# A gated convolution block on one core: y_b's normalization moved behind y_a's last evacuation, and q's lo parts made by ScalarE and an accumulating DMA

## The chip, the cores and the metric

The kernel runs on one core of one Trainium2 chip. The engines named here are TensorE (PE in the profile, its weight loads PEld), VectorE (DVE), ScalarE (ACT), GpSimd (POOL) and SyncE (SP, which only issues DMAs). The metric is the device time of one execution in microseconds; less is better.

## The reference

One layer of a streaming encoder on `x` of 1024 positions by 1024 channels, all in fp32:

- `h` is an RMS norm of `x`, scaled and shifted by a modulation of `c`. One projection of `h` with 7 x 1024 columns gives `b_s, c_s, v_s, v_c, gl_c` and two gates.
- `y_a = (b_s * conv3(c_s * v_s)) @ w_short_out`, with a causal convolution of width 3.
- `u = conv31(v_c * sigmoid(gl_c)) + bias`, then a layer norm over the channels, then `silu`; `y_b = u @ w_conf_out`.
- `x = x + g1 * ((g_a * y_a + g_b * y_b) @ w_o)`, with `g_a`, `g_b` the sigmoids of the gates.
- A second norm and modulation, a SwiGLU feed-forward with 2816 hidden channels, a second residual sum and a last RMS norm.

In the kernel's names `q` is `b_s * conv3(c_s * v_s)`, the operand of y_a, and `zs` is the normalized `silu` that is the operand of y_b.

## The kernel before

Channels lie on the 128 partitions (eight blocks of 128), positions along the free dimension in two halves of 512. The products keep fp32 accuracy by a split: a number is a hi part (rounded to `float32r`) plus a lo part (what the rounding left), and `mm3` issues three matmuls, hi x hi, hi x lo and lo x hi (lines 277, 278 and 280). So every operand is made in two steps: a cast to hi on ScalarE and a subtraction for lo. For weights this is `split_w`: the cast L203, and the lo part L204 on VectorE or, for the window projections and `w_short`, on GpSimd. For activations it is `split` (cast L308, subtraction L309 on VectorE).

The stages, in the order of the program:

1. Norm of `x`, modulation, and a first part of the projection ("lead"), up to about 130 us.
2. The window projections: twelve duals, each two pairs of column blocks for both halves, by seven products (`PRODUCTS`) in place of eight. `win_evac` takes each product out of PSUM. The kinds of a pair are `u` (the GLU), `p` (`c_s * v_s`, then `short_conv`), `q` (b_s times the short convolution) and `g` (gates). VectorE runs the 31-tap convolution (L608) between the evacuations; GpSimd makes the weights' sums (L226 to L230) and lo parts. At the end of each `q` pair, `q_store` runs for two blocks and two halves: ScalarE casts half of `sc[j]` into the first half of a tile `qs` (L491), GpSimd subtracts it to make the lo part in the second half (L492), and SyncE stores `qs` to DRAM (L494). There are four such groups, at about 229 to 248, 331 to 366, 450 to 488 and 547 to 565 us of the span, sixteen stores in all.
3. y_a: for each of eight output blocks `j`, 48 matmuls for both halves; VectorE multiplies each half with its gate into `ma` (L702). Beside it run the layer norm's mean and variance, and `act_b`, which prepares y_b's operand: multiplication with the reciprocal deviation (VectorE, L681), `silu` (ScalarE, L682), and the split (L308, L309).
4. y_b, half by half: `row_blocks` runs over the eight input blocks `k` and keeps eight output blocks open in PSUM, six of the pool `ps`, which y_a uses too, and two of `ps2`. `next_b(k, h)` calls `act_b` one step ahead, and a piece of modulation (L262), whose operand is a DMA of SyncE (`raw<-in_ada`).
5. The output projection "mix", the feed-forward, the last norm.

The order on each engine is fixed when the program is built. The framework's planner goes through the program with estimated times, gives each engine the instruction that is ready and stands earliest in the program, and gives out the slots of the tile pools as they come free. `tc.issue_after(ins)` adds one constraint: what the block issues on the engine of `ins` comes behind `ins` in that engine's order. At run time each engine follows its order and waits where something isn't ready. SyncE's DMAs and GpSimd's DMAs go out in the order of those engines.

`sc`, `qs`, `p`, `u` and the gates' `sig` tiles share the pool `uc`, which has eight slots; a slot is free for the next tile when the last reader of the old one is done.

Of the kernel before, what the change touches and what calls it, by code (L numbers as in the profile page):

```python
# [36 lines left out]
AF = mybir.ActivationFunctionType  # L37
ALU = mybir.AluOpType
# [4 lines left out]
H = 512  # L43
KC = D // P
# [61 lines left out]
def block_kernel(ctx: ExitStack, tc: tile.TileContext, xT, c, vecs, ada, w_first, w_plain, w_duals,  # L106
                 w_short, w_conf, w_o, w_fi, w_fo, w_last, outT):
    nc = tc.nc
# [36 lines left out]
    def s_tile(name, dt=F32):  # L145
        return hl_tile(name, dt)

    def g_tile(name):
        return gsp.tile([P, H], F32, tag="gs", name=name)

    def f32(t):
        return t.bitcast(F32)

    halves = (slice(0, H), slice(H, T))
# [18 lines left out]
    def col(base, k):  # L173
        return vec[:, base + k : base + k + 1]
# [70 lines left out]
    def next_w(ahead=AHEAD):  # L245

        fetch(ahead + 1)
        return ready.pop(0)
# [6 lines left out]
    def modulation(i, raw=None):  # L255

        b = ADA_ORDER[i]
        if raw is None:
            raw = load(ada[i])
        else:  # L260
            nc.sync.dma_start(raw, ada[i])
        nc.vector.tensor_tensor_reduce(  # L262
            out=raw, in0=raw, in1=cs, scale=1.0, scalar=col(V_ADA, b),
            op0=ALU.mult, op1=ALU.add, accum_out=modc(b),
        )
# [16 lines left out]
    def col_block(w, act, hs, name):  # L282

        outs = [ps_tile(f"{name}{h}") for h in hs]
        for k in range(KC):
            mm3(outs, slice(k * P, k * P + P), w, [act[k][h] for h in hs], k == 0, k == KC - 1)
        return outs
# [18 lines left out]
    def split(src, tile_of, name):  # L306
        hi, lo = tile_of(name + "h", dt=F32R), tile_of(name + "l", dt=F32R)
        nc.scalar.copy(hi, src)  # L308
        split.ins = nc.vector.tensor_tensor(lo, src, f32(hi), ALU.subtract).ins  # L309
        return hi, lo  # L310
# [93 lines left out]
    def uc_tile(name, n=T + CK - 1, dt=F32):  # L404
        return ucp.tile([P, T + CK - 1], dt, tag="uc", name=name)[:, :n]
# [78 lines left out]
    sc = [None] * KC  # L484
    q_dram = {}

    def q_store(j):

        for h in range(2):
            s = uc_tile("qs", T, F32R)  # L490
            nc.scalar.copy(s[:, :H], sc[j][:, halves[h]])  # L491
            nc.gpsimd.tensor_tensor(s[:, H:], sc[j][:, halves[h]], f32(s[:, :H]), ALU.subtract)  # L492
            q_dram[j, h] = dram.tile([P, T], F32, name=f"q{j}{h}")
            nc.sync.dma_start(q_dram[j, h], f32(s))  # L494

# [17 lines left out]
    def win_evac(pairs):  # L513
# [15 lines left out]
        def evac(i, m, ps):  # L529
# [22 lines left out]
            elif m == "5":  # L552
                e["z"] = e["c"][1] if kind == "g" else g_tile("z")
                nc.scalar.copy(e["z"], ps)
            elif m == "7":
                plus(e["z"], ps, e["z"])
                if kind in "ug":
                    nc.scalar.activation(e["z"], e["z"], AF.Sigmoid, scale=-1.0)
                elif kind == "q":
                    minus_times(sc[j + 1][:, halves[1]], e["z"], sc[j + 1][:, halves[1]])  # L560
            else:
                if kind in "ug":
                    sig = e["c"][0] if kind == "g" else g_tile("sig")
                    nc.scalar.activation(sig, ps, AF.Sigmoid, scale=-1.0)
                if kind == "u":
                    nc.vector.tensor_tensor(e["b"][0], e["b"][0], sig, ALU.mult)
                elif kind == "p":
                    minus_times(e["b"][0], ps, e["b"][0])
                    short_conv(j, e["p"])
                elif kind == "q":  # L570
                    minus_times(sc[j + 1][:, halves[0]], ps, sc[j + 1][:, halves[0]])
                    for i in range(2):
                        q_store(j + i)
                else:
                    for g, t in zip((j, *rest), e["t"]):
                        nc.scalar.dma_start(gate_dram[g], t)
# [58 lines left out]
    def ln_mean():  # L635
        mu = []
        for h in range(2):
            mps = ps_tile("mu")
            nc.tensor.matmul(mps, ones, tot[h], start=True, stop=True)
            nc.scalar.activation(tot[h], mps, AF.Copy, scale=1.0 / D)  # L640
            mu.append(tot[h])
        return mu
# [3 lines left out]
    def ln_square(j):  # L646
        cv.append(uc_tile(f"cv{j}", T))
        nc.sync.dma_start(cv[j], cv_dram[j])
        for h in range(2):
            nc.vector.tensor_tensor(cv[j][:, halves[h]], cv[j][:, halves[h]], mu[h], ALU.subtract)  # L650
            sq = g_tile("sq")
            nc.scalar.activation(sq, cv[j][:, halves[h]], AF.Square, scale=1.0 / 32.0)
            if j == 0:
                sqs[h] = sq
            else:
                nc.vector.tensor_tensor(sqs[h], sqs[h], sq, ALU.add)

    def ln_rstd(sqs):
        vs, ts = [], []
        for h in range(2):  # L660
            vs.append(ps_tile("var"))
            nc.tensor.matmul(vs[h], ones, sqs[h], start=True, stop=True)
        for h in range(2):
            ts.append(g_tile(f"rl{h}t"))
            nc.scalar.activation(ts[h], vs[h], AF.Ln, bias=eps2)
        return [rstd_end(vs[h], eps2, *exp_half(ts[h], f"rl{h}")) for h in range(2)]
# [11 lines left out]

    def act_b(k, h):
        z = cv[k][:, halves[h]]  # L680
        nc.vector.tensor_tensor(z, z, rl[h], ALU.mult)  # L681
        nc.scalar.activation(z, z, AF.Silu, bias=col(V_LNB, k), scale=col(V_LNG, k))  # L682
        zs[k, h] = split(z, s_tile, "zs")

    def next_b(k, h):

        if (k, h) < (KC - 1, 1):
            act_b(*((k + 1, h) if k < KC - 1 else (0, 1)))
        modulation(24 + KC * h + k)
        return zs[k, h]  # L690
# [5 lines left out]
    ma = {}  # L696
    for j in range(KC):
        for h, ps in enumerate(col_block(next_w(), qT, (0, 1), "ya")):
            ga = g_tile("ga")
            nc.gpsimd.dma_start(ga, gate_dram["a", j][:, halves[h]])  # L700
            ma[j, h] = s_tile(f"ma{j}{h}")
            nc.vector.tensor_tensor(ma[j, h], ps, ga, ALU.mult)  # L702
        if j == 0:
            mu = ln_mean()
        if j < 5:
            for i in range((0, 1, 3, 5, 7)[j], (1, 3, 5, 7, 8)[j]):
                ln_square(i)
        if j == 5:
            rl = ln_rstd(sqs)
        if j == KC - 2:  # L710
            act_b(0, 0)
        if j < KC - 2:
            modulation(16 + j)
# [403 lines left out]
```

## Time and profile before

| | |
|---|---|
| median of 3 runs | 1540.28 us (1537.14 to 1541.44) |
| the profiled execution | 1538.34 us, its span 1536.6 us |
| mean granted TensorE clock | 0.988 |
| TensorE busy | 1470.5 us, 96% of the span |
| VectorE, ScalarE, GpSimd busy | 1182.1, 636.5 and 597.1 us |

A row of the time line gives the start from the beginning of the span, the duration, the engine, the line of the kernel, the operation, the tile written and the tiles read, and the number of instructions merged; in brackets stands the idle time of the engine before it and what ended it. A row of the waits reads: who waited, on whom, microseconds in total, how many times, the longest. A row of the windows gives the stretch, its length, TensorE's busy time and instructions, the granted clock, the share of the DMA engines that was busy, and GB/s. A row by line or tile gives the shortest, median and longest duration in ns, and the first and last start.

### The profile page before, as it was taken

The page shows a single profiled execution, that of the slowest core. Times are in us where ns is not written, and L with a number is a line of the kernel's source. Part 1 is how long each engine was busy: PE and PEld are TensorE (multiplying, and loading weights), DVE is VectorE, ACT ScalarE, POOL GpSimd, SP SyncE. Part 2 cuts the span into 40 slices and gives each one's busy share as a digit, 9 for nine tenths or more (in the row PEclk, how much of TensorE's full clock was granted, in tenths as well). Part 3 has the DMA queues.
Part 4 walks back from the last instruction along what each step waited for, and adds up shares of the span by engine and source line. Part 5 has one row for each costly group of instructions (what it writes and reads, how often), then busy time and mean ns, then how long its engine had stood idle before and what let it go on. Part 6 is the DMA issues. An engine that isn't in the chain of part 4 may idle for free.

```text
span 1536.6 us, 17882 instructions
## 1 busy us (share of the span) xinstructions
PE 1470.5 (96%) x6466; PEld 1206.8 (79%) x6466; DVE 1182.1 (77%) x1559; ACT 636.5 (41%) x894; POOL 597.1 (39%) x493
## 2 busy tenths in 40 slices
PE   4799999999998999999999989999999999999996
PEld 3588887877886888877788868788888888888885
DVE  7987898989998882875975798777767765676756
ACT  6563334333333343244334564444444443212235
POOL 1316788788768884310111101101000016535005
PEclk9999999999999999999999999999999999999998
DMA  9432214223222249754764527544444449999403
GB/s 365 149 103 72 96 56 151 69 97 110 96 69 96 70 175 394 252 185 158 238 208 158 168 80 259 192 151 151 151 152 154 155 151 368 349 297 272 129 14 110
DMA packets 88024, 256.16 MB, mean 167 GB/s; under 512 B 10112, under 2 KB 12288, under 8 KB 87936
## 3 DMA queue, kind: packets, MB, share of 16 engines
q1 hardware_dynamic: 47248, 147.01, 28.4%
q0 software_dynamic: 36944, 95.44, 19.1%
q10 hardware_dynamic: 3744, 12.58, 2.0%
q8 instruction: 50, 0.82, 0.2%
q14 instruction: 38, 0.31, 0.1%
HBM read 188.41 MB, written 66.58 MB: 166 GB/s over the span
## 4 chain that ended last, share of the span: by engine, by line
PE 41%; issue 7%; DVE 2%; DMA 1%; POOL 0%; ACT 0%; DVEq 0%; ACTq 0%; POOLq 0%
PE x L277 6%; PE x L280 6%; PE x L278 6%; PE z L280 3%; PE z L277 3%; PE z L278 3%; PE y L280 2%; PE y L278 2%; PE y L277 2%; PE mix L280 1%; PE mix L278 1%; PE mix L277 1%; PE yb L277 1%; DMA hid<-stage 1%; PE yb L278 1%
## 5 line engine op out<-in xcount | busy, mean ns | idle before, releaser
L203 ACT CAST wh<-raw 128x1024 fp32r<-128x1024 f32 (+2 forms) x260 | 262.0, 1009 | 408.5 <-PE z L278 99.8
L204 POOL TENSOR_TENSOR wl<-raw,wh 128x1024 fp32r<-128x1024 f32 (+1 forms) x95 | 242.7, 2562 | 101.0 <-ACT wh L203 93.2
L204 DVE TENSOR_TENSOR wl<-raw,wh 128x1024 fp32r<-128x1024 f32 (+2 forms) x165 | 189.3, 1148 | 56.0 <-ACT wh L203 53.6
L608 DVE SCALAR_TENSOR_TENSOR c<-diff,vec,c 128x512 f32<-128x512 f32 x248 | 182.3, 750 | 6.4 <-DMA q<-qs 2.6
L868 POOL DMA_DIRECT2D hid<-stage x71 | 37.9, 534 | 352.4 <-DVE stage L317 350.2
L277 PE MATMUL x<-th,wh 128*128 128x512 f32 x336 | 130.7, 389 | 0.0
L278 PE MATMUL x<-tl,wh 128*128 128x512 f32 x336 | 130.7, 389 | 0.0
L280 PE MATMUL x<-th,wl 128*128 128x512 f32 x336 | 130.7, 389 | 0.0
L608 DVE SCALAR_TENSOR_TENSOR c<-u,wsum,c 128x512 f32<-128x512 f32 x112 | 84.0, 750 | 7.1 <-issue 5.1
L277 PE MATMUL x<-t2h,wh 128*128 128x512 f32 x184 | 73.4, 400 | 6.3 <-ACT wh L203 4.5
L280 PE MATMUL x<-t2h,wl 128*128 128x512 f32 x184 | 72.9, 397 | 4.6 <-POOL wl L204 4.1
L262 DVE CUSTOM_DVE_ANT_0 raw<-raw,cs,vec 128x1024 f32<-128x1024 f32 x24 | 34.6, 1444 | 51.2 <-DMA raw<-in_ada 47.0
L277 PEld LDWEIGHTS x<-th,wh 128*128 128x128 f32 x336 | 63.1, 188 | 13.2
L278 PEld LDWEIGHTS x<-tl,wh 128*128 128x128 f32 x336 | 63.1, 188 | 13.1
L280 PEld LDWEIGHTS x<-th,wl 128*128 128x128 f32 x336 | 63.1, 188 | 13.0
L278 PE MATMUL x<-t2l,wh 128*128 128x512 f32 x184 | 72.9, 396 | 0.2
L280 PE MATMUL z<-th,wl 128*128 128x512 f32 x168 | 65.5, 390 | 0.0
L277 PE MATMUL z<-th,wh 128*128 128x512 f32 x168 | 65.4, 389 | 0.0
L278 PE MATMUL z<-tl,wh 128*128 128x512 f32 x168 | 65.4, 389 | 0.0
L316 ACT CAST stage<-g 128x512 fp32r<-128x512 f32 x62 | 38.3, 620 | 60.9 <-DVE g L857 30.4
L894 POOL DMA_DIRECT2D th<-hid x71 | 38.1, 536 | 53.9 <-PE x L280 29.4
L277 PE MATMUL yb<-zsh,wh 128*128 128x512 f32 x128 | 51.2, 400 | 7.4 <-DVE ma L702 6.2
(819 smaller groups left out, 4104.3 us busy)
## 6 DMA issues: line engine op xcount, KB each, us to landing
hid<-stage POOLq DMA_DIRECT2D x71, 512.0 KB, 4.3
raw<-in_w_fi SPq DMA_DIRECT2D x50, 512.0 KB, 4.5
raw<-in_w_duals SPq DMA_DIRECT2D x48, 512.0 KB, 3.5
th<-hid POOLq DMA_DIRECT2D x71, 256.0 KB, 5.9
tl<-hid POOLq DMA_DIRECT2D x71, 256.0 KB, 5.9
ada<-in_ada SPq DMA_DIRECT2D x24, 512.0 KB, 7.6
raw<-in_ada SPq DMA_DIRECT2D x24, 512.0 KB, 4.5
raw<-in_w_fo SPq DMA_DIRECT2D x24, 384.0 KB, 5.9
```

Of the source, the lines that this page charges most:

```text
L203: nc.scalar.copy(wh, raw)
L204: lo = lo_engine.tensor_tensor(wl, raw, f32(wh), ALU.subtract)
L262: nc.vector.tensor_tensor_reduce(out=raw, in0=raw, in1=cs, scale=1.0, scalar=col(V_ADA, b), op0=ALU.mult, op1=ALU.add, accum_out=modc(b),)
L277: nc.tensor.matmul(ps, wh, xh, start=first, stop=False, skip_group_check=again)
L278: nc.tensor.matmul(ps, wh, xl, start=False, stop=False, skip_group_check=again)
L280: mm3.ins = nc.tensor.matmul(ps, wl, xh, start=False, stop=last, skip_group_check=again).ins
L316: nc.scalar.copy(hi, src)
L608: tap.ins = nc.vector.scalar_tensor_tensor(out=out, in0=src[:, s : s + H], scalar=wt, in1=acc, op0=ALU.mult, op1=ALU.add).ins
L868: nc.gpsimd.dma_start(hid_dram[key], s)
L894: nc.gpsimd.dma_start(t, hid_dram[key][:, s])
```

## The change

Two edits, independent of each other.

In `act_b` the multiplication L681 is put behind the last `ma` evacuation (`ma["ins"]`, the L702 of block 7, second half) in VectorE's order, once that evacuation has been issued by the program. The first call, `act_b(0, 0)`, comes before it in the program and stays as it was; the other fifteen are constrained.

In `q_store` the lo part is no longer a subtraction on GpSimd. ScalarE writes the negative of the hi part into the second half of `qs`, and a DMA issued by GpSimd adds the half of `sc[j]` to it in place (`accum_op=ALU.add`). SyncE's store waits for that DMA. What is computed is the same.

```diff
@@ q_store
             s = uc_tile("qs", T, F32R)
             nc.scalar.copy(s[:, :H], sc[j][:, halves[h]])
-            nc.gpsimd.tensor_tensor(s[:, H:], sc[j][:, halves[h]], f32(s[:, :H]), ALU.subtract)
+            nc.scalar.activation(s[:, H:], f32(s[:, :H]), AF.Copy, scale=-1.0)
+            nc.gpsimd.dma_start(s[:, H:], sc[j][:, halves[h]], accum_op=ALU.add)
             q_dram[j, h] = dram.tile([P, T], F32, name=f"q{j}{h}")
             nc.sync.dma_start(q_dram[j, h], f32(s))
@@ act_b
         z = cv[k][:, halves[h]]
-        nc.vector.tensor_tensor(z, z, rl[h], ALU.mult)
+        with ExitStack() as order:
+            if (KC - 1, 1) in ma:
+                order.enter_context(tc.issue_after(ma["ins"]))
+            nc.vector.tensor_tensor(z, z, rl[h], ALU.mult)
         nc.scalar.activation(z, z, AF.Silu, bias=col(V_LNB, k), scale=col(V_LNG, k))
@@ the loop of y_a
             ma[j, h] = s_tile(f"ma{j}{h}")
-            nc.vector.tensor_tensor(ma[j, h], ps, ga, ALU.mult)
+            ma["ins"] = nc.vector.tensor_tensor(ma[j, h], ps, ga, ALU.mult).ins
```

## The prediction

> **What bounds the kernel now.** I read the page's first part, then TensorE's waits, then the time line and the windows around the places they name. The line of busy times says that TensorE is the bound; only its gaps can be won.
>
> ```profile
> PE 1470.5 (96%) x6466; PEld 1206.8 (79%) x6466; DVE 1182.1 (77%) x1559; ACT 636.5 (41%) x894; POOL 597.1 (39%) x493
> ```
>
> The profiled execution took 1538.34 us (span 1536.6), 1.9 us below the median of the runs, 1540.28. TensorE's waits, added up by what ended them, put two things within reach of the diff: one long wait at y_b for a `ma` evacuation, and waits in the window stage for a low part on GpSimd (`wl`), four of them.
>
> ```profile
> PE x L280 <- POOL wl L204: 6.8, 4, 2.7
> ...
> PE yb L277 <- DVE ma L702: 6.2, 1, 6.2
> ```
>
> The time line around the long wait (start, duration, engine, line, tiles; the bracket is idle time and its releaser):
>
> ```profile
> 682.43 1.28 DVE L702 TENSOR_TENSOR ma<-ya,ga 128x512 f32<-128x512 f32 x2
> 683.63 1.22 DVE L204 TENSOR_TENSOR wl<-raw,wh 128x1024 fp32r<-128x1024 f32 x1
> 684.87 0.33 SPq L189 DMA_DIRECT2D raw<-in_ada  x1
> 685.36 1.29 DVE L681 TENSOR_TENSOR cv<-cv,rl0r 128x512 f32<-128x512 f32 x2
> 686.56 1.89 DVE L681 TENSOR_TENSOR cv<-cv,rl1r 128x512 f32<-128x512 f32 x3
> 687.97 0.39 PE L280 MATMUL yb<-zsh,wl 128*128 128x512 f32 x1
> 689.63 1.28 DVE L262 CUSTOM_DVE_ANT_0 raw<-raw,cs,vec 128x1024 f32<-128x1024 f32 x1 [1.18 <-DMA raw<-in_ada]
> 690.85 3.09 DVE L681 TENSOR_TENSOR cv<-cv,rl1r 128x512 f32<-128x512 f32 x5
> 693.86 1.28 DVE L702 TENSOR_TENSOR ma<-ya,ga 128x512 f32<-128x512 f32 x2
> 694.60 0.79 PE L277 MATMUL yb<-zsh,wh 128*128 128x512 f32 x1 [6.24 <-DVE ma L702]
> ```
>
> Before the gap y_b has run four of its eight output blocks, twelve matmuls or 2.6 us (at 25 in 5.40 us, below), until 688.3; so y_a's last block left TensorE at about 685.6. The fifth needs a PSUM bank that y_a's last block still holds. VectorE frees it with the two L702 of 693.86, but ahead of them in its order stand ten multiplications (L681) and a modulation that waits for its load. The windows show what follows a gap: the same 5.40 us hold 13 matmuls at a granted clock of 0.50, then 25 at 1.00; after a 2.7 us gap at 490.3 it is 9 and then 17 in 3.40 us.
>
> ```profile
> 694.60:700.00 5.40, 5.40 (x13) 0.50 0.75 222
> 700.00:705.40 5.40, 5.40 (x25) 1.00 0.34 114
> 492.00:495.40 3.40, 3.40 (x9) 0.53 0.83 265
> 496.00:499.40 3.40, 3.40 (x17) 1.00 0.42 145
> ```
>
> So the long gap cost 6.2 + 5.4 x (1 - 13/25) = 6.2 + 2.6 = 8.8 us, and a gap of some 2.5 us carries 3.4 x (1 - 9/17) = 1.6 us more. [...]
>
> **Part one, the multiplications behind `ma`.** The rows of y_b's preparation (shortest, median and longest ns, first and last start):
>
> ```profile
> L681 DVE TENSOR_TENSOR cv<-cv,rl0r x8: 685/689/692, 677.6 to 686.0; 128x512 f32<-128x512 f32 x8
> L682 ACT ACTIVATE cv<-cv,vec x16: 798/802/818, 678.3 to 695.9; 128x512 f32<-128x512 f32 x16
> L308 ACT CAST zsh<-cv x16: 604/616/618, 683.0 to 758.1; 128x512 fp32r<-128x512 f32 x16
> L309 DVE TENSOR_TENSOR zsl<-cv,zsh x16: 681/687/694, 684.8 to 763.9; 128x512 fp32r<-128x512 f32 x16
> ```
>
> Nothing is added or removed; 15 of the 16 L681 (all but the first, which is issued before the last block's `ma` exists) may no longer stand ahead of the last L702 on VectorE. What can still stand there is the lo part at 683.63, the one of the first `zs`, and the modulation. The modulation's load was issued at 684.87, when the lo part at 683.63 had freed its buffer, and its use began at 689.63. Six of the eight multiplications that start from 677.6 to 686.0 stood ahead of 683.63 (two are those of 685.36), and five of them go; at 0.6 us each that brings all this up to 3 us forward, the modulation to about 687. Then the two L702 (1.28) end between 686.9 (not behind the modulation) and 689.6 (behind it); TensorE wants the bank at 688.3. I take 0.5 us of remaining wait, bounds 0 and 1.3, too short for the clock to fall.
>
> What is late next: y_b's second k needs `zs` of k=1, whose chain starts only now: 0.69 + 0.80 + 0.62 + 0.69 = 2.8 us from the end of `ma`; meanwhile TensorE has four blocks of three matmuls, 12 x 5.4/25 = 2.6 us. So it fits within a few tenths. Each later k gives 24 matmuls, 5.2 us, against 1.4 us of multiplication and lo part, 1.2 of weight lo part and 1.3 of modulation. The other multiplications thus lie beside matmuls; without that cover, 14 more of 0.69 would cost 9 us. GpSimd's `gb` loads, whose slots the last multiplications free, have until the evacuations of y_b, eight k of 5.2 us later. Part one: 8.8 - 0.5 = 8.3 us gained, bounds 6 and 8.8.
>
> **Part two, q's lo parts.** Sixteen subtractions on GpSimd become sixteen negatives on ScalarE, sixteen DMA issues on GpSimd, and sixteen transfers of 256 KB that must land before SyncE's store and before the slots of `sc` come free.
>
> ```profile
> L492 POOL TENSOR_TENSOR qs<-sc,qs x16: 1283/1304/2274, 229.4 to 563.9; 128x512 fp32r<-128x512 f32 x16
> L700 POOL DMA_DIRECT2D ga<-gate_a x16: 538/538/730, 541.1 to 678.0; - x16
> DMA to landing us min/median/max: 3.1/3.9/6.7
> L752 POOL DMA_DIRECT2D x_dram<-x x16: 542/547/547, 792.3 to 872.5; - x16
> DMA to landing us min/median/max: 2.3/2.9/5.5
> ga<-gate_a POOLq DMA_DIRECT2D x2, 256.0 KB, 4.6
> q<-qs SPq DMA_DIRECT2D x16, 512.0 KB, 2.6
> ```
>
> ScalarE: a negative costs about what the cast L308 does over the same 128x512; 16 x 0.62 = 9.9 us on an engine that is 41% busy, hidden in its idle time; without that at most these 9.9. GpSimd: 16 x (1.30 - 0.54) = 12.2 us of its in-order time come free. That matters where a weight's lo part stands behind the subtractions and TensorE waits for it:
>
> ```profile
> 363.46 3.00 POOL L492 TENSOR_TENSOR qs<-sc,qs 128x512 fp32r<-128x512 f32 x2
> PE x L280 <- POOL wl L204: 1.4, 1, 1.4
> 483.43 4.50 POOL L492 TENSOR_TENSOR qs<-sc,qs 128x512 fp32r<-128x512 f32 x2
> 487.90 7.02 POOL L204 TENSOR_TENSOR wl<-raw,wh 128x1024 fp32r<-128x1024 f32 x3
> PE x L280 <- POOL wl L204: 2.7, 1, 2.7
> ```
>
> (The two waits are those of the windows 365 to 372 and 486 to 494.) Two issues take 1.1 us, so the lo parts come 1.9 and 3.4 us sooner: both waits go, 1.4 + 2.7 and 1.6 of clock, 5.7 us. The other waits for `wl` (6.8 - 1.4 - 2.7 = 2.7 us) I let stay.
>
> Against it stand the slots. No row shows an accumulating transfer; its landing L is bounded by the rows of GpSimd's 256 KB transfers, from 2.3 us (the quickest store L752) to 6.7 (the slowest load L700). I take 4.0, between the loads' median 3.9 and the 4.6 of the two that are issued inside the window stage, the nearest in place. [...] In the first group of q stores the slots already hold VectorE up:
>
> ```profile
> 238.86 1.30 POOL L492 TENSOR_TENSOR qs<-sc,qs 128x512 fp32r<-128x512 f32 x1
> 242.86 0.62 ACT L491 CAST qs<-sc 128x512 fp32r<-128x512 f32 x1 [1.69 <-DMA q<-qs]
> 244.95 2.56 POOL L492 TENSOR_TENSOR qs<-sc,qs 128x512 fp32r<-128x512 f32 x2
> 247.58 0.72 DVE L608 SCALAR_TENSOR_TENSOR c<-u,wsum,c 128x512 f32<-128x512 f32 x1 [5.13 <-issue]
> 251.63 0.74 ACT L621 ACTIVATE u<-c,vec 128x512 f32<-128x512 f32 x1 [5.67 <-DVE c L608]
> 252.88 0.50 PE L277 MATMUL x<-t2h,wh 128*128 128x512 f32 x1 [0.37 <-ACT u L539]
> ```
>
> VectorE idles 5.1 us until 247.58, just after the last subtraction ends (247.51): the next `u` takes a slot of `sc`. Behind it in ScalarE's order comes the copy (L539) that TensorE waits for. After: the second transfer, issued at 238.9, lands at 238.9 + L; its store (0.1 to issue, 2.6) at 241.6 + L; then the fourth cast and negative (1.2) and the issue at 242.9 + L; landed at 242.9 + 2L, that is 2L - 4.6 us later than 247.5. With L = 4.0 TensorE's gap grows by 3.4 us, past 2.5, so 1.6 of clock come on top: 5.0 us lost. With 2.3 it is nothing, with 6.7 it is 8.8 + 1.6 = 10.4. What stands behind the stores on SyncE's queue are the weight loads, and these wait for weight buffers anyway:
>
> ```profile
> SPq L189 <- POOL wl L204: 357.6, 49, 28.3
> ```
>
> 49 loads wait 357.6 us in all, 7 each, so I cost a store that issues later at nothing; without that cover, up to L each. Part two: 5.7 - 5.0 = 0.7 us gained; bounds 5.7 gained and 4.7 lost.
>
> **The sum.** 8.3 + 0.7 = 9.0 us: 1538.3 - 9.0 = 1529.3 against the profiled execution, which is 1531 on the scale of the median.
>
> **The rivals.** (1) *The transfer is quick or the order absorbs it*: L from 2.3 to 3, at most 1.4 lost at the first stores; 8.3 + 4.3 to 5.7 gained, about 1527. For it: SyncE's store of twice the bytes lands in 2.6 us there. Against: those 4.6. (2) *The stall forms again one step later*: the planner lays all 15 multiplications in one row ahead of the first lo part, as it laid 2, 3 and 5 in a row above; 15 x 0.6 + 0.7 = 9.7 us, and TensorE, wanting `zs` of k=1 2.6 us after `ma`, waits 7 us again, with 2.6 of clock. Part one gains nothing, about 1540 with the 0.7 of part two: no change. Against it: by the code the `zs` tiles share a pool with q's 32, which y_a reads to its end; by then they are free, and a lo part that is ready stands earlier in the program. (3) *`ma` stays behind the modulation, which comes no sooner*: use from 689.6 to 690.9, the first `ma` at 691.6, a wait of 3.3 plus 1.6 of clock; gain 3.9 instead of 8.3, about 1536. (4) *Slower: the accumulating transfer lands late*, as it reads two streams and may be slow in the DMA engines. Its place is the slots of the first stores, its price 2L - 4.6 and 1.6. At L = 8.5 that is 14.0 and eats all the gain (5.7 + 8.3); at L = 11 it is 19.0, 5.0 us slower than before, about 1545. For it: VectorE's wait of 5.1 us shows that this place has no slack left. Against it: the longest row is 6.7.
>
> **How the numbers follow.** Forecast 0.46, (1) 0.16, (2) 0.13, (3) 0.08, (4) 0.17. A measurement here tells about 0.3%, 4.6 us, from no change. Faster, below 1535.7: 0.46 + 0.16 and 0.05 of (3), 0.67. Same: (2) and the other 0.03, 0.16. Slower: (4), 0.17. The range 1524 to 1541 takes in (1) to (3) and leaves (4) out; the forecast's own is 1526 to 1535.
>
> **What would show it.** Right: no TensorE wait for `ma`; clock 1.00 from 690 to 705; L702 of the last block within some 3 us of 686; the waits for `wl` near 368 and 490 gone; a longer VectorE idle near 247 and a TensorE gap near 253 of 3 to 4 us. Wrong: a TensorE wait of several us for `zsh` or `zsl` at y_b; accumulating transfers that land after 6 us or more; ScalarE or VectorE waits for slots in all four groups; SyncE's weight loads late behind the stores, shown as GpSimd or ScalarE waiting for `raw`.

## The result and the profile after

| | before | after |
|---|---|---|
| median | 1539.36 us (1535.5 to 1541.44, 6 runs) | 1562.61 us (1556.85 to 1564.72, 6 runs) |
| the profiled execution, its span | 1538.34, 1536.6 us | 1564.72, 1562.7 us |
| mean granted TensorE clock | 0.988 | 0.984 |

The ratio is 1.0152, 95% interval 1.0137 to 1.0167. The kernel became 23 us slower where 9 us less was forecast; 1562.6 is 21 us above the upper end of the range, 1541. Gains and losses in us below are differences of medians; the kernel before, timed beside each run, had medians from 1537.0 to 1539.4 us, so they are good to some 2 us.

The first line of the page of the changed kernel, and then TensorE's waits from 215 to 640 us, the window stage and y_a's start (before, the only waits of note there were the 6.8 and 1.2 us for `wl`):

```profile
PE 1474.9 (94%) x6466; PEld 1209.0 (77%) x6466; DVE 1200.2 (77%) x1559; ACT 645.5 (41%) x910; POOL 583.9 (37%) x493
```

```profile
PE ya L277 <- ACT wh L203: 9.9, 1, 9.9
PE x L277 <- ACT p L540: 6.7, 2, 4.5
PE x L280 <- POOL wl L204: 4.8, 3, 2.4
PE x L277 <- DVE z L508: 3.6, 1, 3.6
PE x L277 <- ACT u L540: 2.7, 1, 2.7
PE x L277 <- ACT sig L540: 2.4, 1, 2.4
PE x L277 <- DVE sig L508: 1.5, 1, 1.5
```

The wait for `ma` at y_b is gone. In its place stand a wait of 9.9 us at y_a's first matmul and six others of 1.5 to 4.5 us in the window stage, beside the three for `wl`. Where the 26.1 us of span came from, by the first matmul of each stage (every dual is named by its start before and after; a dual without loss takes 38.1 us):

| stage | before | after | change |
|---|---|---|---|
| up to the dual at 238.3 / 239.1 | 238.3 | 239.1 | +0.8 |
| dual 238.3 / 239.1 (first q stores) | 39.5 | 45.2 | +5.7 |
| dual 277.8 / 284.3 | 38.0 | 38.0 | 0 |
| dual 315.8 / 322.3 | 40.1 | 38.1 | -2.0 |
| dual 355.9 / 360.4 | 39.8 | 46.0 | +6.2 |
| the two duals from 395.7 / 406.4 | 76.2 | 76.2 | 0 |
| dual 471.9 / 482.6 | 46.9 | 46.1 | -0.8 |
| dual 518.8 / 528.7 | 38.1 | 44.4 | +6.3 |
| dual 556.9 / 573.1, with the wait at y_a | 38.0 | 48.1 | +10.1 |
| y_a, from 594.9 / 621.2 | 90.5 | 93.8 | +3.3 |
| y_b, from 685.4 / 715.0 | 97.9 | 90.8 | -7.1 |
| from mix to the end | 753.3 | 756.9 | +3.6 |

3.4 us of the last row are one gap of TensorE that nothing in the profile releases; I don't count it as the change's. Three of the duals as windows of the changed kernel (length; TensorE busy; clock, DMA share and GB/s at the end):

```profile
239.10:284.30 45.20, 40.37 (x170) 32.54 (x169) 35.57 (x55) 17.68 (x25) 34.84 (x17) 0.96 0.44 134
360.40:406.40 46.00, 40.15 (x169) 32.43 (x168) 44.28 (x51) 15.62 (x23) 32.82 (x18) 0.96 0.33 99
573.10:621.20 48.10, 38.24 (x169) 31.34 (x167) 19.20 (x27) 18.43 (x29) 20.86 (x12) 0.92 0.91 314
```

The clock of 0.96 in the first two comes from the stretches behind their gaps (0.57 from 258.01 to 261.41, 0.54 from 388.49 to 391.89), that of 0.92 from the wait at y_a itself (0.61 from 611.30 to 621.20; behind it, 0.50 from 621.24 to 624.64). In the dual at 360.4 VectorE is busy for 44.28 of 46.0 us (37.95 of 39.8 before), although it has less to do in number (51 instructions instead of 56): something in it became longer.

The place where the prediction saw the loss, the first group of q stores (ScalarE's and VectorE's time lines):

```profile
248.72 0.62 ACT L491 CAST qs<-sc 128x512 fp32r<-128x512 f32 x1 [4.36 <-DMA qs<-sc]
257.38 0.59 ACT L540 COPY u<-x 128x512 f32<-128x512 f32 x1 [4.14 <-DMA qs<-sc]
...
251.78 0.06 DVE L524 MEMSET p<- 128x2 f32 x1 [3.88 <-DMA q<-qs]
257.44 0.08 DVE L409 MEMSET u<- 128x30 f32 x1 [3.63 <-DMA qs<-sc]
```

ScalarE and VectorE wait for the accumulating transfer and the store behind it, and ScalarE's copies for TensorE (L540) stand behind that. The transfers themselves, by the line that issues them (durations of the issue in ns; to landing, shortest, median, longest):

```profile
L493 POOL DMA_DIRECT2D qs<-sc x16: 856/894/1482, 232.3 to 580.8; - x16
DMA to landing us min/median/max: 3.3/4.2/7.5
```

The second place is a surprise. VectorE's two longest instructions, and what GpSimd ran meanwhile:

```profile
369.01 9.44 DVE L567 TENSOR_TENSOR u<-u,sig 128x512 f32<-128x512 f32 x1
494.43 9.06 DVE L501 SCALAR_TENSOR_TENSOR sc<-p,vec,sc 128x1024 f32<-128x1024 f32 x1
...
368.78 2.04 POOL L493 DMA_DIRECT2D qs<-sc  x2
369.92 7.97 POOL L204 TENSOR_TENSOR wl<-raw,wh 128x1024 fp32r<-128x1024 f32 x3
493.25 2.06 POOL L493 DMA_DIRECT2D qs<-sc  x2
494.40 8.01 POOL L204 TENSOR_TENSOR wl<-raw,wh 128x1024 fp32r<-128x1024 f32 x3
```

The same multiplication of 512 elements took 1.12 us before:

```profile
362.92 1.12 DVE L566 TENSOR_TENSOR u<-u,sig 128x512 f32<-128x512 f32 x1
```

Here it ends at 378.45, just after GpSimd's third lo part (377.89); the tap ends at 503.49, just after the row of 494.40 (502.41). Shortly ahead of each, VectorE had waited for a slot that an accumulating transfer held, 0.93 and 5.72 us:

```profile
366.76 0.06 DVE L524 MEMSET p<- 128x2 f32 x1 [0.93 <-DMA qs<-sc]
493.77 0.06 DVE L524 MEMSET p<- 128x2 f32 x1 [5.72 <-DMA qs<-sc]
```

So slots were held in the groups of stores behind the first too, and these waits are part of what set the moment at which VectorE met GpSimd's rows; no run takes them away alone.

The third place is y_a's first weight. ScalarE's wait for it, SyncE's queue after, and then the same part of the queue before:

```profile
ACT wh L203 <- DMA raw<-in_w_short: 7.1, 1, 7.1
...
611.36 0.32 SPq L585 DMA_DIRECT2D q71l<-q  x1
612.72 2.36 SPq L189 DMA_DIRECT2D raw<-in_w_short  x3
```

```profile
567.56 0.33 SPq L189 DMA_DIRECT2D raw<-in_w_short  x1
568.01 0.36 SPq L584 DMA_DIRECT2D q00h<-q  x1
```

Before, y_a's first weight was loaded ahead of the 32 loads of q; after, the planner put it behind all of them. These loads also went out later. All but the first of them stand behind the last two q stores, and the last store waited for a transfer that was issued at 580.77 and landed at 588.32, the slowest of the sixteen:

```profile
583.84 4.84 SPq L495 DMA_DIRECT2D q<-qs  x2
```

At y_b the evacuations of `ma` now end 1.3 us after the last y_a block, and the clock stays at 1.00 (VectorE, and the window that answers the one at half clock before):

```profile
715.01 1.29 DVE L706 TENSOR_TENSOR ma<-ya,ga 128x512 f32<-128x512 f32 x2 [1.30 <-PE ya L280]
```

```profile
715.00:720.40 5.40, 5.40 (x25) 4.46 (x25) 5.39 (x9) 4.02 (x6) 1.07 (x2) 1.00 0.73 243
```

### The profile page after: what moved, and what is told of

Read it like the earlier page. It is cut to its first block, busy times and chain, and to the rows that moved or that the text cites. A ratio compares the mean times of both kernels' runs of the same rounds, so it can differ in the third digit from the quotient of the medians.

```text
span 1562.7 us, 17909 instructions
## 1 busy us (share of the span) xinstructions
PE 1474.9 (94%) x6466; PEld 1209.0 (77%) x6466; DVE 1200.2 (77%) x1559; ACT 645.5 (41%) x910; POOL 583.9 (37%) x493
## 4 chain that ended last, share of the span: by engine, by line
PE 71%; DVE 19%; issue 3%; DMA 3%; POOL 2%; ACT 2%; SPq 0%; DVEq 0%; ACTq 0%; POOLq 0%
PE x L280 9%; PE x L277 9%; PE x L278 9%; DVE c L609 8%; PE z L277 5%; PE z L278 5%; PE z L280 5%; PE y L277 3%; PE y L280 3%; PE y L278 3%; DVE sc L501 2%; PE ya L280 2%; PE mix L278 2%; PE mix L277 2%; PE mix L280 2%
## 5 line engine op out<-in xcount | busy, mean ns | idle before, releaser
L203 ACT CAST wh<-raw 128x1024 fp32r<-128x1024 f32 (+2 forms) x260 | 262.0, 1009 | 406.4 <-PE z L278 99.0
L280 PEld LDWEIGHTS x<-th,wl 128*128 128x128 f32 x336 | 63.3, 189 | 13.4
L317 DVE TENSOR_TENSOR stage<-g,stage 128x512 fp32r<-128x512 f32 x62 | 42.5, 688 | 24.8 <-ACT stage L316 24.7
```

The source lines that it names most:

```text
L203: nc.scalar.copy(wh, raw)
L280: mm3.ins = nc.tensor.matmul(ps, wl, xh, start=False, stop=last, skip_group_check=again).ins
```

## The experiments

**Part one alone.** The subtraction of q's lo part stays on GpSimd, as before.

```diff
-            nc.scalar.activation(s[:, H:], f32(s[:, :H]), AF.Copy, scale=-1.0)
-            nc.gpsimd.dma_start(s[:, H:], sc[j][:, halves[h]], accum_op=ALU.add)
+            nc.gpsimd.tensor_tensor(s[:, H:], sc[j][:, halves[h]], f32(s[:, :H]), ALU.subtract)
```

> Part one alone: the multiplications behind the last `ma`, q's lo parts as before. My theory (part one does what was forecast, part two makes the loss): TensorE's 6.2 us wait for `ma` and its slow clock go, nothing new appears, 8 us faster than before, about 1531 us. Rival (part one costs too, because the operands of y_b come late): a wait of several us at y_b's second k, within 3 us of before.

Measured: 1534.39 us, ratio 0.9979 (0.9964 to 0.9994); 3.7 us gained against 1538.06 in the same job. VectorE at y_b's start and at the middle of y_b, then TensorE there:

```profile
685.71 1.28 DVE L262 CUSTOM_DVE_ANT_0 raw<-raw,cs,vec 128x1024 f32<-128x1024 f32 x1 [4.87 <-DMA raw<-in_ada]
686.92 1.28 DVE L705 TENSOR_TENSOR ma<-ya,ga 128x512 f32<-128x512 f32 x2
...
733.32 2.35 DVE L204 TENSOR_TENSOR wl<-raw,wh 128x1024 fp32r<-128x1024 f32 x2
735.59 0.68 DVE L309 TENSOR_TENSOR mg10l<-gb,mg10h 128x512 fp32r<-128x512 f32 x1
736.19 0.68 DVE L736 TENSOR_TENSOR gb<-yb,gb 128x512 f32<-128x512 f32 x1
...
736.93 0.50 PE L277 MATMUL yb<-zsh,wh 128*128 128x512 f32 x1 [3.13 <-DVE gb L736]
```

The wait for `ma` falls from 6.24 to 1.3 us: the modulation still stands ahead and waits 4.87 us for its load. y_b's first half takes 45.9 us instead of 52.6 (43.5 in the changed kernel, which has no wait in that half): of the 2.4 us over the latter the wait leaves 1.1, where the half clock (0.50) had cost 2.6 before. But where the second half begins, TensorE wants a bank that VectorE frees late: modulations and two weights' lo parts stand ahead of the evacuations (L736) in its order. This wait of 3.13 us, with a clock of 0.68 behind it (736.93 to 740.33), makes y_b's second half 3.6 us longer than before.

**The late modulations.** Part one alone, and the last two modulations of each half of y_b issued behind that half's evacuations.

```diff
-        modulation(24 + KC * h + k)
+        if k < KC - 2:
+            modulation(24 + KC * h + k)
...
         for o in range(KC - 4, KC):
             join(o, h, gs[o])
+        modulation(24 + KC * h + KC - 2)
+        modulation(24 + KC * h + KC - 1)
```

> Only the order of the multiplications, as in the kernel that came out at 0.9979 of the one before, and the last two modulations of each half of y_b placed behind its evacuations. Theory (part one gave 3.1 us and some clock back at the middle of y_b, because a modulation that waits for its load and two weights' lo parts stood ahead of the evacuations on VectorE): the wait for gb at 736.93 falls below 1.5 us and the time is 3 to 5 us under that kernel's, about 1530, 0.995 of the kernel before. Rival (the load of the weights or the gb loads bound that place): the wait stays and the time is 1534.

Measured: 1529.7 us, ratio 0.9938 (0.9921 to 0.9955). TensorE has no wait for `gb` left; of y_b's waits only this one is over 0.5 us:

```profile
PE yb L277 <- DVE ma L706: 1.2, 1, 1.2
```

y_b takes 89.2 us (684.2 to 773.4) against 97.9 before: 8.7 us. Of these 7.0 lie in y_b's first half (45.7 us against 52.6), where part one works, and 1.7 in the second half, which had waited 1.1 us for `gb` before. This kernel is faster than the kernel before and than part one alone.

**Part two alone.** `act_b` as before.

```diff
-        with ExitStack() as order:
-            if (KC - 1, 1) in ma:
-                order.enter_context(tc.issue_after(ma["ins"]))
-            nc.vector.tensor_tensor(z, z, rl[h], ALU.mult)
+        nc.vector.tensor_tensor(z, z, rl[h], ALU.mult)
```

> Part two alone: ScalarE's negative and the accumulating DMA, the multiplications where they were. My theory: both parts add up, so the changed kernel's 1562.6 plus the 8 us of part one, about 1570 us; the window stage, from the first dual to y_a's first matmul, as long as in the changed kernel (496 us against 471). Rival (the loss comes from both parts together): well under 1562.

Measured: 1558.66 us, ratio 1.0131 (1.011 to 1.0151). The loss is all part two's. And here y_b doesn't wait for `ma` either, although the ten multiplications stand ahead again. The modulation's load was issued at 708.34, 6.6 us ahead of y_b's start at 714.91 (before, 0.6 us ahead), it landed at 712.84, and the evacuation at 717.18 comes in time.

```profile
712.96 1.28 DVE L262 CUSTOM_DVE_ANT_0 raw<-raw,cs,vec 128x1024 f32<-128x1024 f32 x1 [1.04 <-issue]
714.17 3.09 DVE L682 TENSOR_TENSOR cv<-cv,rl1r 128x512 f32<-128x512 f32 x5
717.18 1.28 DVE L703 TENSOR_TENSOR ma<-ya,ga 128x512 f32<-128x512 f32 x2
```

So the gains of the two parts don't add: behind part two there is nothing left for part one to remove. Part one even costs y_b 1.8 us there (90.8 in the changed kernel, 89.0 here), by waits for `gb` of 3.1 instead of 1.0 us at the middle.

**The addition on GpSimd.** The changed kernel with the negative on ScalarE and GpSimd adding `sc` to it, no transfer.

```diff
-            nc.gpsimd.dma_start(s[:, H:], sc[j][:, halves[h]], accum_op=ALU.add)
+            nc.gpsimd.tensor_tensor(s[:, H:], sc[j][:, halves[h]], f32(s[:, H:]), ALU.add)
```

> The changed kernel with ScalarE's negative, but GpSimd adds in place of the DMA, so no transfer has to land before the slots come free. My theory (the transfer's landing holds the slots of `sc` and `qs`): the window duals are again as long as before, within 4 us; what is left is the wait at y_a's first matmul, as the planner puts the first `w_short` load behind the q loads here too, 10 to 13 us with its clock: about 1543 us. Rival (the negative on ScalarE, or the planner's new order, makes the loss): about 1560 us, with the waits in the window stage still there.

Measured: 1544.44 us, ratio 1.004 (1.0028 to 1.0053). 18 of the 23 us go with the transfer. What is left must come from the negatives and the order that the planner made around them; the two weren't told apart. The time is near the 1543 that was expected, but by another sum: y_a waits only 3.2 us for its first weight, which stands behind the q loads here too, and the dual of the first q stores takes 42.6 us, 3.1 more than before, though no transfer has to land in it.

**A plain copy.** The transfer stays, without the accumulation; every engine's order is the changed kernel's.

```diff
-            nc.gpsimd.dma_start(s[:, H:], sc[j][:, halves[h]], accum_op=ALU.add)
+            nc.gpsimd.dma_start(s[:, H:], sc[j][:, halves[h]])
```

> The changed kernel with a plain DMA of the same 256 KB in place of the accumulating one: the addition is left out, so q's lo part holds q itself and the output is not the reference's. Every engine's order is the same as in the changed kernel. If adding in the DMA engines makes the transfers slow: the landing falls from a median of 3.4 us to about 2.5 and most of the window stage's 25 us come back, 1545 us or less. If any transfer in that place costs this: landing within 0.3 us of 3.4 and the time within 4 us of 1562.6.

Measured: 1546.61 us, ratio 1.0057 (1.0038 to 1.0076). The copies:

```profile
L493 POOL DMA_DIRECT2D qs<-sc x16: 527/567/720, 231.8 to 567.6; - x16
DMA to landing us min/median/max: 2.3/3.0/6.0
```

(The median of 3.4 us in the expectation had SyncE's stores mixed in; the accumulating transfers alone have 4.2.) Accumulating costs 0.33 us more per issue and 1.2 us more to landing, and the kernel pays 16 us for it. In the first group the size agrees with the forecast: 2L - 4.6 is 1.4 us for L = 3.0, and that dual took 41.2 us (238.6 to 279.8), 1.7 over the 39.5 of before; but with no transfer at all it lost 3.1, so the sum isn't shown by this. At y_a's first matmul the wait is still 8.3 us. But sixteen times 1.5 us, most of it hidden, is not 16 us. What differs in the dual at 355.9, which takes 38.1 us here and 46.0 in the changed kernel, is the multiplication L567: VectorE reached it before the row of lo parts, and it took 1.27 us. (The other gap, 3.6 us for `z`, stays here; GpSimd's row of three lo parts before it ran from 482.41 to 489.52.)

**A transfer that only holds `sc`.** Part one alone, and a copy of each half of `sc` to DRAM by GpSimd, on which no store waits.

```diff
             nc.gpsimd.tensor_tensor(s[:, H:], sc[j][:, halves[h]], f32(s[:, :H]), ALU.subtract)
+            nc.gpsimd.dma_start(dram.tile([P, H], F32, name=f"hold{j}{h}"), sc[j][:, halves[h]])
```

> Part one alone (q's lo parts by GpSimd's subtraction, as before), with one more DMA of GpSimd in each of the sixteen stores, which copies the half of `sc` to DRAM: the slot of `sc` is held until that lands, while `qs` and its store wait for nothing new. My theory (held slots): VectorE again waits at the memsets of `p` and `u`, and the window stage grows by some 5 to 10 us over part one alone, to about 1538. Rival (only the longer way of `qs` to its store, or the planner's place of the weight load, counts): within 3 us of part one alone, apart from 16 x 0.54 us of GpSimd's time.

Measured: 1548.46 us, ratio 1.0068 (1.0042 to 1.0095), 14 us over part one alone, where the theory had 5 to 10 and the rival 3; the profiled execution, 1543.59 us, is the quickest of the four. The transfers land in 2.4 us (median). VectorE waits for them twice, 6.1 us in the first group, where it had waited 5.1 before, and 2.4 us at 489: the waits for held slots alone don't make the loss. The dual that begins at 355.9 takes 50.0 us, and two VectorE instructions near it are as long as GpSimd's rows beside them (the first row has a subtraction, a lo part, two sums and one of the weights' sums):

```profile
354.70 9.08 DVE L601 TENSOR_TENSOR diff<-u 128x526 f32<-128x526 f32 x1
369.84 7.96 DVE L567 TENSOR_TENSOR u<-u,sig 128x512 f32<-128x512 f32 x1
```

So the long instruction needs neither the accumulation nor the wait of a store. A DMA issue of GpSimd stands directly ahead of each of these rows, here as in the changed kernel.

**A memset behind each lo part.** The changed kernel, with a break in GpSimd's rows.

```diff
+    gap = fill.tile([P, 256], F32, name="gap")
...
             pool_los.append(lo.ins)
+            with tc.issue_after(lo.ins):
+                nc.gpsimd.memset(gap, 0.0)
```

> The changed kernel, with one small memset (128x256, it reads no SBUF) on GpSimd behind every lo part of a dual's weights; every other order is the changed kernel's but for a few neighbours. In the changed kernel two VectorE instructions with two SBUF inputs last as long as GpSimd's whole row of three lo parts beside them: the multiplication u<-u,sig at 369.01 took 9.44 us and the tap sc<-p,vec,sc at 494.43 took 9.06 us; the gaps of 4.50 us at 388.49 (for p) and 3.57 at 522.95 (for z) come some 20 us later. Theory (VectorE is shut out for as long as GpSimd's instructions follow each other without a break): with the memsets both fall to at most about 4 us, the gaps of 4.5 and 3.6 go with their clock, and the kernel gains 8 to 12 us against the changed kernel, about 1552. Rival (the two gaps come from the slots that the accumulating transfers hold): the gaps stay at 3.5 us or more and the time stays within 3 us of 1562.

Measured: 1566.22 us, ratio 1.0171 (1.0154 to 1.0188): a miss. The memsets open nothing; VectorE is shut out through three lo parts and three memsets (VectorE, then GpSimd):

```profile
374.22 7.60 DVE L567 TENSOR_TENSOR u<-u,sig 128x512 f32<-128x512 f32 x1
...
375.35 3.32 POOL L204 TENSOR_TENSOR wl<-raw,wh 128x1024 fp32r<-128x1024 f32 x1
377.67 1.25 POOL L206 MEMSET gap<- 128x256 f32 x1
377.94 3.32 POOL L204 TENSOR_TENSOR wl<-raw,wh 128x1024 fp32r<-128x1024 f32 x1
```

The long instructions stayed, and so did the gaps (5.0 us for `p`, 3.58 for `z`), so the run doesn't tell the theories apart. GpSimd itself is not slowed: its records overlap here, and a lo part and a memset together take 2.59 us from one start to the next, where three lo parts without memsets took 7.97.

**One input from SBUF.** The changed kernel, every order the same; the two instructions read one SBUF operand.

```diff
@@ win_evac
-                    nc.vector.tensor_tensor(e["b"][0], e["b"][0], sig, ALU.mult)
+                    if j == 5:
+                        nc.vector.tensor_reduce(e["b"][0][:, :1], sig, mybir.AxisListType.X, ALU.add)
+                    else:
+                        nc.vector.tensor_tensor(e["b"][0], e["b"][0], sig, ALU.mult)
@@ short_conv
+            if (j, s) == (6, 1):
+                nc.vector.tensor_reduce(sc[j][:, :1], p[:, s : s + T], mybir.AxisListType.X, ALU.add)
+                continue
             nc.vector.scalar_tensor_tensor(
```

> The changed kernel with every engine's order as it was; only the two VectorE instructions that lasted 9.44 us (u<-u,sig at 369.01) and 9.06 us (the first tap of sc at 494.43) are replaced in place by a reduction that reads one SBUF input, sig and p, and writes one column; that one multiplication and that one tap are left out of the output. [...] Theory (these two, shut out by GpSimd's rows of lo parts, make the gaps of 4.50 us at 388.49 and 3.57 us at 522.95): both take under 2 us, both gaps go, and the kernel gains the 6.2 and 6.3 us that the duals from 360.4 and from 528.7 lost, 10 to 13 us, about 1551. Rival (the slots held by the accumulating transfers make the gaps, and the long instructions only fill time that VectorE had): the gaps stay above 2.5 us and the time stays above 1558.

Measured: 1549.19 us, ratio 1.0068 (1.0048 to 1.0087): 13.4 us less than the changed kernel (VectorE, and the dual as a window):

```profile
369.46 0.68 DVE L567 TENSOR_REDUCE u<-sig 128x1 f32<-128x512 f32 x1
489.17 1.21 DVE L501 TENSOR_REDUCE sc<-p 128x1 f32<-128x1024 f32 x1
491.75 6.52 DVE L501 SCALAR_TENSOR_TENSOR sc<-p,vec,sc 128x1024 f32<-128x1024 f32 x1
```

```profile
360.80:400.60 39.80, 38.35 (x169) 31.45 (x168) 38.07 (x56) 16.74 (x24) 34.81 (x19) 1.00 0.40 126
```

Both gaps are gone, although VectorE still waits 5.70 us for a slot at 488.51; so it is the long instructions that made them. The dual at 360 is back at 39.8 us, all of its 6.2. The second place was put down wrongly in part: the dual that ended with the 3.57 us gap gains 3.3 us (42.8 instead of 46.1; the next tap is now shut out for 6.52 us), while the dual behind it keeps its loss (45.5 us against 38.1 before). At y_a's first matmul 9.7 us are gained, and that is what these two instructions account for; the rest came from mix on, most of it the unexplained gap there, which this execution doesn't have. Measured are the 0.68 us in place of 9.44 and, beside one row of lo parts (489.11 to 497.18), the 1.21 us of the reduction and the 6.52 of the next tap, which ended at 498.27. A reduction differs from what it replaces in its operation and output too, so that the second SBUF input decides is the author's reading and was not shown by this run alone; the taps in the last section fit it.

**y_a's weight first.** The changed kernel, with the q loads issued behind the load of y_a's first weight.

```diff
-            if d == n_duals - 1:
-                for n in range(4 * i, min(4 * i + 4, 2 * KC)):
-                    q_load(n // 2, n % 2)
+            if d == n_duals - 1 and i == 4:
+                fetch(AHEAD + 1)
+                with tc.issue_after(load.ins):
+                    for n in range(2 * KC):
+                        q_load(n // 2, n % 2)
```

> The changed kernel with all q loads put behind the first load of `w_short` on SyncE, as they stood before the change. My theory (TensorE's 9.9 us wait at y_a's first matmul, and 2.9 us of slow clock after it, come from that load's place on SyncE's queue): the wait goes or shrinks below 3 us, about 1550 us; the window stage before it as in the changed kernel. Rival (q's operands themselves are late, and the weight load only seems to be the releaser): the wait stays near 10 us, then for `q00h`, and the time near 1562.

Measured: 1552.17 us, ratio 1.0087 (1.0065 to 1.0108): 10.4 us gained. y_a's wait of 9.9 us becomes one of 0.9, and y_b starts 12.6 us earlier (702.4 against 715.0); that the clock of 0.50 behind the wait goes with it is an estimate, from these 12.6 against the 9.0 of the wait. y_b then takes 94.6 us instead of 90.8, with 2.1 us for `ma` at its start and 2.5 us for `gb` at its middle, the places that part one alone had shown.

**Combinations.** The memsets with y_a's weight first:

> The memsets and the earlier load of y_a's first weight together on the changed kernel. If the two losses are separate, as the places say (window stage, and y_a's first matmul), the gains add: 1562.6 less 10.4 less 8 to 12, that is 1540 to 1545, close to the kernel before; what then remains is the first group's loss of 5 to 6 us and the half boundary of y_b. If the waits trade with each other, about 1550.

Measured: 1556.28 us, ratio 1.0118 (1.0098 to 1.0138), above both expectations and 4 us over y_a's weight first alone, as the memsets cost it there too. Then the two reductions with y_a's weight first:

> The two reductions in place of the shut-out instructions and y_a's first weight load ahead of the q loads, together on the changed kernel; one multiplication and one tap are again left out of the output. Each alone gave 13.4 and 10.4 us. If the two account for separate losses, the time is 1562.6 - 23.8 = 1538.8, within 3 us, level with the kernel before: then these two explain the excess, and what the slots of sc still cost (5.7 us in the dual at 239.1, some in the last but one) is about what part one gives at y_b (7.1 us there). If the earlier start of the last duals runs into the weights or the q transfers, it is 1542 to 1549.

Measured: 1543.14 us, ratio 1.0037 (1.0026 to 1.0049). Together 19.5 us instead of 23.8, outside the 3 us. Up to y_a's first matmul the two do add: 19.7 us earlier than in the changed kernel, against 9.7 and 10.5 alone. y_b takes 94.9 us instead of 90.8, but it took 94.6 with y_a's weight first alone, so the 10.4 us hold that already. The missing 4 us lie from mix on, where the profiled execution of the changed kernel took 756.9 us and the three repaired ones 751.8, 754.2 and 752.6: both single gains had been credited with that difference. The two causes are separate and account for most of the 23 us; y_a still begins 6.6 us later than before (601.55 against 594.95).

## Why the prediction was wrong, step by step

**What bounds the kernel.** Right: what was lost or gained shows as gaps of TensorE and the clock behind them, which was 0.50 to 0.57 behind four of those of the changed kernel (258.01, 388.49, 545.04 and 621.24). The price of that clock was too simple: see the last section.

**Part one.** The long wait and its cause were right, and so was its price of 8.8 us: y_b's first half took 52.6 us before and takes 43.5 without a wait. What part one left there was 2.4 us, not 0.5: a wait of 1.3, the upper bound, since the modulation came ahead of `ma`, and 1.1 more behind it. So its gain in that half was 6.7 us (7.0 with the late modulations), not 8.3; that y_b gained 8.7 in the end is the middle's doing. Two things were missed. "What is late next" looked at y_b's second k and at its last evacuations, not at the middle, where the faster first half runs into evacuations that stand behind modulations and lo parts (3.6 us given back). And "Part one: 8.3 us gained" was worked out in the kernel of before, then added to part two: with part two the wait isn't there.

**Part two, the terms that held.** A negative takes 0.626 us (0.62 forecast); that it hides wasn't shown, see the addition on GpSimd. The transfer lands after 4.2 us in the median (4.0), though the slowest took 7.5. The first group lost 5.7 us (5.0), close partly by luck: the second transfer was issued at 245.37, not 238.9, the last two landed after 5.5 and 6.5 us, and TensorE lost its time in two gaps, 2.18 and 2.65 us, with a clock of 1.00 behind the first (252.34 to 255.74) and 0.57 behind the second (258.01 to 261.41). The issue takes 0.89 us, not 0.54, the price of a plain one.

**Part two, the waits for `wl`.** "Both waits go" failed: 1.34 us stayed at 373.26, and 1.0 of 2.7 at 497.77. In the first place the two issues took 2.04 us, not 1.1, and GpSimd reached them 8.4 us into the dual instead of 7.5, which ate nearly all of the 1.9 us. In the second the lo part came sooner, but TensorE wanted it sooner too: the wait ahead of it (2.38 us at 485.56) had a clock of 1.00 behind it (to 488.96), the one of before (2.48 us at 474.98) 0.53 (to 478.38).

**Part two, the step that failed most.** The groups of q stores behind the first and SyncE's queue were costed at nothing, "without that cover up to L each". In two later groups VectorE waited for held slots (0.93 and 5.72 us) and then met GpSimd's rows of lo parts with instructions that have two SBUF inputs: 9.7 us up to y_a by the reductions. And the weight loads were taken to wait for buffers anyway; the planner put y_a's first one behind 32 loads, of which all but one stood behind the last transfer's landing: 10.1 us up to y_a's first matmul and 3.3 us in y_a, of which 10.4 came back with the repair. The landing has a part in this: from the same place on the queue the wait was 3.2 us with no transfer, 8.3 with the plain copy and 9.9 with the accumulating one. But the price is not one L, as the sentence on the missing cover had it; it is the length of what VectorE ran into and the place of a load. No rival named either: (4) had the sign, but put it into the slots of the first group and asked for L of 11 us, where the median was 4.2.

**What stays open.** The dual that begins at 528.7 loses 6.3 us to two waits for `sig` (2.43 and 1.49 us) and the clock of 0.52 behind the first (545.04 to 548.44), and 4.8 with the plain copy, but nothing with the addition on GpSimd or with the copies to DRAM. There VectorE's order has convolution taps ahead of these evacuations; which step of the planner put them so wasn't isolated. Nor is it settled why two of the sixteen transfers took over 6 us to land.

## What to carry to other kernels

In a kernel like this one, where the new transfers took 1.2 us longer to land than plain copies and cost 16 us more, a transfer can cost more by what it shifts than by its own wait: list which VectorE instructions have two SBUF inputs and which GpSimd rows they will fall on, and price a meeting at the length of the row (6.5 to 9.4 us here). Price a removed wait in the kernel that will be there after the whole change, not before it; and at every change of an order that a planner makes, look at the queue of loads for the first operand of the next stage.

## What the runs showed of the hardware

- Before, the multiplication `u<-u,sig`, which has two SBUF inputs, took 2.88 us in the four of its five places where it met a GpSimd lo part, until that one ended; at 208.08 it got in after the first of two lo parts that followed each other. In the places above such instructions took 6.5 to 9.4 us, until a whole row of three to five GpSimd instructions had ended, memsets between them included. Each of these rows began right behind a DMA issue of GpSimd; whether that is the reason was not tried. VectorE's instructions with one input in PSUM were not held up: the 368 convolution taps took at most 0.76 us in both kernels and the 72 additions of the window stage (`z<-x,z` and the like) at most 0.69. Beside the row of three lo parts from 487.90 to 494.92 of the kernel before, three taps took 2.06 us together (from 489.54).
- The clock behind a gap doesn't follow its length alone. Windows of the changed kernel behind gaps of 2.65, 3.57 and 2.43 us (clock 0.57, 1.00 and 0.52):

```profile
258.01:261.41 3.40, 3.40 (x9) 2.66 (x10) 3.33 (x6) 2.10 (x3) 2.75 (x3) 0.57 0.94 246
522.95:526.35 3.40, 3.40 (x15) 2.65 (x15) 3.33 (x5) 1.61 (x4) 2.30 (x1) 1.00 0.01 2
545.04:548.44 3.40, 3.40 (x8) 2.69 (x9) 3.26 (x6) 0.90 (x1) 3.40 (x2) 0.52 0.13 14
```

  With the plain copy the same gap of 3.57 us was followed by 0.54 (510.05 to 513.45).
- An accumulating transfer of 256 KB within SBUF took 0.89 us to issue and 4.2 us to land, a plain copy of the same 0.57 and 3.0, a copy of the same `sc` to DRAM 0.56 and 2.4 (medians of 16).
